# The start of a two-layer encoder kernel: first input half and first weights in two transfers each, idle TensorE on a zero tile, first half transposed in two parts

## Chip, core and metric

The kernel runs on one core of a Trainium2 chip. The metric is device time in microseconds (us) of one execution. Three runs of the kernel before gave 914.66, 915.12 and 915.35 us; their median, 915.12 us, is the time that the changed kernel is held against.

## What is computed

Two layers over x of 256 tokens by 1024 columns, fp32. Each layer has three sublayers, each followed by a layer norm of the scaled input plus the sublayer's output: a SwiGLU block, a mixer (chunked mLSTM in layer 0, windowed attention in layer 1), and a second SwiGLU block.

```python
for l in range(DEPTH):                                    # DEPTH = 2
    x = layer_norm(ALPHA * x + 0.5 * swiglu(x, ffn_w_in[l, 0], ffn_w_out[l, 0]), ln_g[l, 0], ln_b[l, 0])
    y = mlstm_mixer(x, ...) if l % 2 == 0 else window_attention(x, ...)
    x = layer_norm(ALPHA * x + y, ln_g[l, 1], ln_b[l, 1])
    x = layer_norm(ALPHA * x + 0.5 * swiglu(x, ffn_w_in[l, 1], ffn_w_out[l, 1]), ln_g[l, 2], ln_b[l, 2])
```

Only the first sublayer's beginning matters here: `x @ ffn_w_in[0, 0]`, whose right side has 1024 rows and 5632 columns.

## The kernel before

**Products.** The tokens are two tiles of 128: tile 0 and tile 1. TensorE needs x with its columns on the partitions, so each block of 128 tokens by 128 columns is transposed by a product with the identity (`ident`), and the result is copied out of PSUM. The eight column blocks are numbered k = 0 to 7; k 0 to 3 are the first half of x (columns 0 to 511) and k 4 to 7 the second.

To keep fp32 accuracy every operand is a pair: a high part rounded to fp32r (`xT_hi`, `w_hi`), and a low part that is the raw value less the high part (`xT_lo`, `w_lo`). A product is three matmuls: high by high, low by high, high by low. ScalarE (ACT) casts the high part of a weight piece, VectorE (DVE) subtracts to get the low part.

**Weights.** A piece is 256 rows by 512 columns (128 partitions by 1024 elements in SBUF, two k blocks), 512 KB. Pieces are numbered w0, w1, w2 and so on in order of use. SyncE (SP) issues their transfers through `Weights.load` (L221) and `Paced.load` (L109). There are four buffers (`RAW_BUFS`), so w4's transfer waits for the low part of w0 (`Weights.low`, L322), which frees its buffer.

**The start.** `load_x` (L574) loads x in four transfers of 256 KB, by token tile and half, all issued by ACT. SP issues w0 to w3 at the same time (L582 to L588). Then ACT loads its activation table (L589), and GpSimd's iota and a DVE compare make the identity (L593, L594).

`ffn` then records (L777 to L782): 14 transposes of the identity, whose results nobody reads (`warm`, L656); the four transposes of tile 0's first half, their copy to `xT_hi` and the subtraction for `xT_lo` on DVE (`to_xT`, L648); the split of w0 in two halves of 512 columns (L310 and L329); and eight more idle transposes.

`first_mm` (L802) orders the products of the first two pieces into the first PSUM bank pair, tile 0 and tile 1 of the tokens. For w0, in the order of the code: tile 0 high by `w_hi`; transposes of tile 1's first half; tile 0 low by `w_hi`; tile 0 high by `w_lo`; then the same three products of tile 1. Each of these is two matmuls of 128x512, one for each k block of the piece. For w1 the transposes of the second half of both token tiles come first, then again twelve matmuls. w2 and w3, which need the second half of x, follow through `b_mm` (L796), where each k block's three matmuls stand together, high by low second.

**What sets the order.** Each engine runs its instructions in the order in which they were recorded. `Paced` (L63) keeps a small model of the engines' and the transfers' times while it records; `Weights.fill` (L374) asks that model when to place the next cast or subtraction of a weight piece between other work. A change in the recorded loads or in the model's arrival times can therefore change the order of work on ACT and DVE.

Of the kernel before, what the change touches and what calls it, by code (L numbers as in the profile page):

```python
# [9 lines left out]
F32 = mybir.dt.float32  # L10
FR = mybir.dt.float32r
# [6 lines left out]
S = 256  # L18
# [20 lines left out]
XP = [4, 0, 1, 2]  # L39
LC = [0, 0, 0, 0, 0, 1]  # L40
TD = [2, 3, 2, 0, 2, 1]
MP = [1, 0, 0, 0, 1, 0, 1, 1, 0, 0, 0, 0, 2, 2, 2]
PD = [7, 0, 6, 6, 5]
PEND = [6, 4, 6, 6, 6]
# [9 lines left out]
ISSUING = 450.0  # L54
LANDING = 2200.0
LOADING = 1360.0
# [6 lines left out]
class Paced:  # L63
# [42 lines left out]
                self.there[ap.name][:a.size] = a  # L106
        self.there[ap.name][i] = t

    def load(self, ap, source, engine=None):  # L109
        if engine is not None:  # L110
            engine.dma_start(ap, source)
        elif isinstance(source, list):
            for k, src in enumerate(source):
                self.nc.sync.dma_start(ap[:, k].rearrange("p (m f) -> p m f", m=src.shape[1]), src)
        else:
            self.nc.sync.dma_start(ap, source)
        self.moving(0, ap, LANDING, LOADING * int(np.prod(ap.shape[1:])) / 1024, ISSUING)
# [69 lines left out]
class Weights:  # L187
# [33 lines left out]
    def load(self, most=None):  # L221

        nc = self.nc
        n = 0
        once = False
        while most is None or n < most:
            next_ = []
            for tag, todo in self.todo.items():
                if not todo:
                    continue  # L230
                first = self.first[todo[0]]
                if tag != "w_raw":
                    if self.free[tag] and not once and first < self.used + self.span:
                        next_.append((first, tag, tag))
                elif self.free[tag]:
                    next_.append((first, tag, tag))
                elif todo[0] < self.send and self.free["v_raw"]:
                    next_.append((first, tag, "v_raw"))
            if not next_:
                break  # L240
            _, tag, in_ = min(next_)
            once = once or tag != "w_raw"
            i = self.todo[tag].pop(0)
            pool, bufs = {"w_raw": (self.pool, RAW_BUFS), "v_raw": (self.spool, V_RAW)}.get(in_, (self.rooms, S_RAW))
            t = pool.tile([128, D], F32, name=tag, tag=in_, bufs=bufs)
            nc.load(t.rearrange("p (k f) -> p k f", k=self.words[i]["k"]), self.words[i]["src"])
            self.raw[i], self.words[i]["in"] = t, in_
            self.free[in_] -= 1
            n += 1
# [27 lines left out]
    def next(self, act):  # L277

        nc = self.nc
        free = RING - (len(self.made) - self.gone)  # L280
        i = self.first_left()
        best, need = None, 0
        for n in range(1, LOOK + 1):
            while i in self.made:
                i += 1
            if i >= len(self.plan) or need > free - 1:
                break
            p = self.plan[i]
            if (p["word"] in self.raw and nc.when(self.raw[p["word"]]) < act + SOON
                    and (p["needs"] is None or p["needs"] in self.made)  # L290
                    and not any(p["needs"] == x for x in [h[0] for h in self.half] + [s_[0] for s_ in self.sums])):
                if best is None or p["due"] < self.plan[best]["due"]:
                    best = i
            need = max(need, n - max(0, i - self.gone - n + 1 - KEPT))
            i += 1
        return best
# [146 lines left out]
def trunk_kernel(ctx: ExitStack, tc: tile.TileContext, x, ffn_w_in, ffn_w_out, ln_g, ln_b, ml_w_in, ml_gate_b,  # L443
                 ml_norm_g, ml_w_out, at_w_in, at_sink, at_w_out, out):
    nc = Paced(tc.nc)
    consts = ctx.enter_context(tc.tile_pool(name="consts", bufs=1))
# [78 lines left out]
    for j, (kind, l, i, _) in enumerate(stages):  # L525
        if kind == "ffn":
# [13 lines left out]
            for g in range(SEVENS):  # L540
                c0 = 768 + 512 * g
# [29 lines left out]

    xt = [state.tile([128, D], F32, name=f"x{t}", tag=f"x{t}") for t in range(2)]

    def load_x(t, h):  # L574
        s_ = slice(h * 512, h * 512 + 512)
        nc.load(xt[t][:, s_], x[0, t * 128:(t + 1) * 128, s_], nc.nc.scalar)

    xT = (state.tile([128, 8, S], FR, name="xT_hi", tag="xT_hi"),
          state.tile([128, 8, S], FR, name="xT_lo", tag="xT_lo"))

    W = Weights(nc, wpool, rooms, words, plan, after)
    load_x(0, 0)  # L582
    W.load(1)
    load_x(1, 0)
    W.load(1)
    load_x(0, 1)
    load_x(1, 1)
    W.load()  # L588
    nc.scalar.preload_act_table(AF.Silu)  # L589

    ident = consts.tile([128, 128], F32, name="ident")
# [28 lines left out]
    def pair(p, *idx):  # L620
        return p[0][idx], p[1][idx]
# [4 lines left out]
    def ybank(shape=(128, 512)):  # L626
        return psum.tile(list(shape), F32, name="py", tag="py", bufs=4)
# [3 lines left out]
    def tok(t):  # L631
        return slice(t * 128, (t + 1) * 128)

    def split_evac(dst, src, scale=None, high=None, wait=False):
        if scale is None:
            (high or nc.scalar.copy)(dst[0], src)
            low = lambda: nc.vector.tensor_sub(dst[1], src, dst[0].bitcast(F32))
            if wait:
                W.when_ready(low, dst[0])
            else:  # L640
                low()
        else:
            nc.scalar.activation(dst[0], src, AF.Copy, scale=scale)
            nc.vector.scalar_tensor_tensor(dst[1], src, scale, dst[0].bitcast(F32), op0=OP.mult, op1=OP.subtract)

    turned = {}

    def to_xT(t, src, bank, halves=range(2), high=None):  # L648
        for h in halves:
            p = bank((128, 4, 128))  # L650
            for k in range(4):
                nc.tensor.transpose(p[:, k], src[:, (4 * h + k) * 128:(4 * h + k + 1) * 128], ident)
            split_evac(pair(xT, A, slice(4 * h, 4 * h + 4), tok(t)), p, high=high)
            turned[t, h] = p

    def warm(n):  # L656

        p = ybank((128, 4, 128))
        for j in range(n):
            nc.tensor.transpose(p[:, j % 4], ident, ident)  # L660

    def load_ln(room, l, n):
        t = []
# [50 lines left out]
    def tail(y, h, todo, first, norm, last, turn_at, between=None, rooms_=None):  # L714
# [39 lines left out]
        if rooms_ is not None:  # L754
            norm[0].gb.clear()
            W.back(rooms_, 2)
        W.done(most=TD[bound[0]])
        W.owed, W.landed = 0, False
# [6 lines left out]
    def ffn(l, i, n, pending, last):  # L765
        with ExitStack() as ph:
# [9 lines left out]

            start = pending is None  # L777
            if start:
                warm(14)
                to_xT(0, xt[0], ybank, (0,), nc.vector.tensor_copy)  # L780
                W.split(1)
                warm(8)  # L782
            hs, pieces = [], []

            def tr(hB, t, h):
# [15 lines left out]

            def first_mm(ps, a):  # L802

                def mm(t, i, j):
                    for k in (2 * a, 2 * a + 1):
                        nc.tensor.matmul(ps[t], xT[i][:, k, tok(t)], pieces[a][j][:, k % 2], start=i == j == k == 0,
                                         stop=False)

                if a == 1:
                    for t in range(2):  # L810
                        to_xT(t, xt[t], ybank, (1,))
                pieces.extend(W.take(1))
                mm(0, 0, 0)
                if a == 0:
                    to_xT(1, xt[1], ybank, (0,))
                    W.split(2)
                mm(0, 1, 0)
                if a == 0:
                    mm(0, 0, 1)
                mm(1, 0, 0)  # L820
                if a == 0:
                    mm(1, 0, 1)
                mm(1, 1, 0)
                if a == 1:
                    mm(0, 0, 1)
                    mm(1, 0, 1)

# [39 lines left out]
            if start:  # L867
                sg = {}
                for m in range(2):
                    ps = [wbank(), wbank()]  # L870
                    for a in range(4):
                        if m == 0 and a < 2:
                            first_mm(ps, a)
                        for t in range(2):
                            if m or a > 1:
                                b_mm(ps[t], t, m, a)
                            if m == 1 and a == 3:
                                b_mul(sg[t], ps[t])
# [170 lines left out]
    def mlstm(l, n, pending, last):  # L1049
        with ExitStack() as ph:  # L1050
# [209 lines left out]

            pump = iter(MP)
            spare = lambda: W.done(0, next(pump))
# [351 lines left out]
```

## Time and profile before

| What | Value |
|---|---|
| Three timed runs | 914.66, 915.12, 915.35 us |
| The profiled execution's own time | 914.5 us |
| Its span in the profile | 912.8 us |
| Mean granted clock of TensorE | 0.999 |
| TensorE matmul busy | 903.3 us, 99% of the span, 4459 matmuls |
| VectorE busy | 804.5 us, 88% |
| ScalarE busy | 573.8 us, 63% |

How to read its rows. In the timeline the columns are start and duration in us from the span's start, engine, source line, operation, output<-inputs with shape, and the number of like instructions merged in the row; a bracket tells the engine's idle time before it and what ended that. PE is TensorE's matmuls, PEld its weight loads, ACTq and SPq the issuing of transfers. Most compute instructions pass through one wrapper and so carry its line, L178; they are told apart by the names of their tiles. A matmul's duration includes its way through the array, and the next one starts before it ends; the pitch, start to start, is what counts. In the rows of transfers the last figure is the time from issue to landing.

### The profile page before, as it was taken

How to read it: one execution, taken by the hardware profiler on the slowest of the kernel's cores; microseconds unless marked ns; L12 is line 12 of the kernel's file. 1: busy time of each engine (PE TensorE's matmuls, PEld its weight loads, DVE VectorE, ACT ScalarE, POOL GpSimd, SP SyncE). 2: the span in 40 equal slices, each digit the busy share in tenths (PEclk: the TensorE clock that was granted, in tenths of full speed). 3: DMA queues.
4: the chain of work that ended last, by engine and by line, in shares of the span. 5: the costliest groups of instructions: out<-in, count | busy, mean ns of one | idle time of the engine just before them, and what ended most of it. 6: DMA issues, size and time to landing. Idle time of an engine off the chain costs nothing.

```text
span 912.8 us, 12565 instructions
## 1 busy us (share of the span) xinstructions
PE 903.3 (99%) x4459; PEld 757.8 (83%) x4459; DVE 804.5 (88%) x969; ACT 573.8 (63%) x793; POOL 153.9 (17%) x194
## 2 busy tenths in 40 slices
PE   9999999999999999999999999999999999999996
PEld 7888888889988888888888888888888888888885
DVE  5999999886799898999888899998869889899986
ACT  5786767356664666776646676764569566676660
POOL 0111123013211011211011111110425301111110
PEclk9999999999999999999999999999999999999999
DMA  8999998546637898998868889985434487799851
GB/s 281 361 331 260 287 279 213 164 133 195 199 121 242 287 235 247 287 270 248 239 191 276 254 256 287 265 225 197 160 118 140 162 290 221 201 294 283 255 138 47
DMA packets 100703, 208.53 MB, mean 228 GB/s; under 512 B 6904, under 2 KB 21264, under 8 KB 100640
## 3 DMA queue, kind: packets, MB, share of 16 engines
q1 hardware_dynamic: 82368, 173.04, 54.0%
q0 software_dynamic: 17696, 33.65, 22.1%
q10 hardware_dynamic: 576, 1.05, 0.3%
q8 instruction: 35, 0.57, 0.2%
q14 instruction: 28, 0.23, 0.1%
HBM read 206.65 MB, written 1.05 MB: 228 GB/s over the span
## 4 chain that ended last, share of the span: by engine, by line
PE 95%; DVE 3%; issue 1%; POOL 1%; ACT 0%; DMA 0%; DVEq 0%; POOLq 0%; ACTq 0%
PE pw L178 61%; PE py L178 34%; DVE h L178 1%; POOL hrs L1237 0%; DVE w_lo L178 0%; DMA w_raw<-in_ml_w_out_dram 0%; DVE wt L178 0%; DVE x L178 0%; DVE hst L178 0%; ACT w_hi L178 0%; DVE stats L178 0%; DVE a_lo L178 0%; DVE hmv L178 0%; ACT a_hi L178 0%; DVE q_lo L178 0%
## 5 line engine op out<-in xcount | busy, mean ns | idle before, releaser
L178 DVE TENSOR_TENSOR w_lo<-w_raw,w_hi 128x1024 fp32r<-128x1024 f32 (+1 forms) x213 | 254.9, 1218 | 25.2 <-ACT w_hi L178 23.4
L178 ACT CAST w_hi<-w_raw 128x1024 fp32r<-128x1024 f32 (+1 forms) x213 | 219.0, 1050 | 76.8 <-PE py L178 21.9
L178 DVE TENSOR_TENSOR w_lo<-s_raw,w_hi 128x1024 fp32r<-128x1024 f32 x192 | 228.6, 1219 | 19.4 <-ACT w_hi L178 19.4
L178 ACT CAST w_hi<-s_raw 128x1024 fp32r<-128x1024 f32 x192 | 196.5, 1054 | 59.4 <-PE py L178 23.0
L178 PE MATMUL pw<-w_hi,xT_hi 128*128 128x512 f32 x480 | 189.3, 396 | 0.0
L178 PE MATMUL pw<-w_hi,xT_lo 128*128 128x512 f32 x480 | 186.8, 390 | 0.0
L178 PE MATMUL pw<-w_lo,xT_hi 128*128 128x512 f32 x480 | 186.6, 390 | 0.0
L120 POOL DMA_DIRECT2D s_raw<-in_ffn_w_in_dram x64 | 77.4, 1211 | 484.5 <-DVE s_raw L178 231.5
L178 PE MATMUL py<-w_hi,h_hi 128*128 128x512 f32 x349 | 138.1, 396 | 0.0
L178 PE MATMUL py<-w_hi,h_lo 128*128 128x512 f32 x349 | 136.1, 390 | 0.0
L178 PE MATMUL py<-w_lo,h_hi 128*128 128x512 f32 x349 | 135.8, 389 | 0.0
L178 PEld LDWEIGHTS pw<-w_hi,xT_lo 128*128 128x128 f32 x480 | 90.0, 188 | 19.1
L178 PEld LDWEIGHTS pw<-w_lo,xT_hi 128*128 128x128 f32 x480 | 90.3, 188 | 18.7 <-DVE w_lo L178 1.1
L178 PEld LDWEIGHTS pw<-w_hi,xT_hi 128*128 128x128 f32 x480 | 90.0, 188 | 17.3
L178 PE MATMUL pw<-w_hi,S_hi 128*128 128x512 f32 x256 | 99.6, 389 | 0.0
L178 PE MATMUL pw<-w_lo,S_hi 128*128 128x512 f32 x256 | 99.6, 389 | 0.0
L178 PE MATMUL pw<-w_hi,S_lo 128*128 128x512 f32 x256 | 99.6, 389 | 0.0
L178 PEld LDWEIGHTS py<-w_hi,h_lo 128*128 128x128 f32 x349 | 65.5, 188 | 14.1
L178 DVE TENSOR_TENSOR s_raw<-s_raw,s_raw 128x1024 f32<-128x1024 f32 x64 | 76.8, 1219 | 0.3
L178 PEld LDWEIGHTS py<-w_lo,h_hi 128*128 128x128 f32 x349 | 65.6, 188 | 12.9
L178 PEld LDWEIGHTS py<-w_hi,h_hi 128*128 128x128 f32 x349 | 65.6, 188 | 12.8
L178 PEld LDWEIGHTS pw<-w_hi,S_lo 128*128 128x128 f32 x256 | 48.0, 188 | 10.0
(203 smaller groups left out, 1128.9 us busy)
## 6 DMA issues: line engine op xcount, KB each, us to landing
s_raw<-in_ffn_w_in_dram SPq DMA_DIRECT2D x96, 512.0 KB, 7.9
w_raw<-in_ffn_w_out_dram SPq DMA_DIRECT2D x88, 512.0 KB, 6.0
w_raw<-in_ffn_w_in_dram SPq DMA_DIRECT2D x64, 512.0 KB, 5.5
s_raw<-in_ffn_w_in_dram POOLq DMA_DIRECT2D x64, 512.0 KB, 8.2
w_raw<-in_ml_w_in_dram SPq DMA_DIRECT2D x24, 512.0 KB, 4.4
w_raw<-in_ffn_w_in_dram SPq DMA_DIRECT2D x32, 256.0 KB, 5.8
w_raw<-in_at_w_in_dram SPq DMA_DIRECT2D x12, 512.0 KB, 4.4
w_raw<-in_ml_w_out_dram SPq DMA_DIRECT2D x8, 512.0 KB, 4.2
```

The source lines that it names most:

```text
L120: self.nc.gpsimd.dma_start(ap, source, accum_op=OP.add)
L178: r = f(out, *args, **kw)
```

## The change

- `load_x` takes columns and an engine. The first half of token tile 0 comes in two transfers of 256 columns (128 KB each), still issued by ACT. The other three quarters of x are now issued by SP, between the weights: w0, tile 1 first half, w1, tile 0 second half, w2, tile 1 second half, w3.
- w0 comes in two transfers of 256 KB, one for each k block.
- `warm` now does matmuls of 128x256 on a tile of zeros, `idle`, that DVE fills as its first instruction: 11 before the first transposes of x and 4 after them, in place of 14 and 8 transposes of the identity.
- The four transposes of token tile 0's first half are followed by two copies to `xT_hi` of two blocks each, and the subtraction for `xT_lo` is in two parts as well: k 0 and 1, then the low part of w0, then k 2 and 3.
- `first_mm` for w0: k 0 of tile 0 (high, low) by `w_hi`, then tile 1's transposes, then k 1, then the rest as before.

```diff
+WARM = [11, 4]
-    def load(self, ap, source, engine=None):
-        if engine is not None:
-            engine.dma_start(ap, source)
+    def load(self, ap, source, parts=False):
+        if parts:
+            for k in range(ap.shape[1]):
+                self.nc.sync.dma_start(ap[:, k], source[:, k])
...
-            nc.load(t.rearrange("p (k f) -> p k f", k=self.words[i]["k"]), self.words[i]["src"])
+            nc.load(t.rearrange("p (k f) -> p k f", k=self.words[i]["k"]), self.words[i]["src"], i == 0)
...
-    load_x(0, 0)
+    idle = consts.tile([128, S], FR, name="idle")
+    nc.vector.memset(idle.bitcast(F32), 0.0)
+    load_x(0, 0, 256, nc.nc.scalar)
+    load_x(0, 256, 512, nc.nc.scalar)
     W.load(1)
-    load_x(1, 0)
+    load_x(1, 0, 512, nc.nc.sync)
     W.load(1)
-    load_x(0, 1)
-    load_x(1, 1)
+    load_x(0, 512, 1024, nc.nc.sync)
+    W.load(1)
+    load_x(1, 512, 1024, nc.nc.sync)
     W.load()
...
-        p = ybank((128, 4, 128))
+        p = ybank((128, S))
         for j in range(n):
-            nc.tensor.transpose(p[:, j % 4], ident, ident)
+            nc.tensor.matmul(p, idle[:, 0:128], idle, start=True, stop=True)
...
-                warm(14)
-                to_xT(0, xt[0], ybank, (0,), nc.vector.tensor_copy)
-                W.split(1)
-                warm(8)
+                warm(WARM[0])
+                p = turned[0, 0] = ybank((128, 4, 128))
+                ks = slice(0, 2), slice(2, 4)
+                for k in range(4):
+                    nc.tensor.transpose(p[:, k], xt[0][:, k * 128:(k + 1) * 128], ident)
+                    if k % 2:
+                        nc.vector.tensor_copy(xT[0][:, ks[k // 2], tok(0)], p[:, ks[k // 2]])
+                warm(WARM[1])
+                W.high(0)
+                for i in range(2):
+                    nc.vector.tensor_sub(xT[1][:, ks[i], tok(0)], p[:, ks[i]], xT[0][:, ks[i], tok(0)].bitcast(F32))
+                    if i == 0:
+                        W.low()
...
                 if a == 0:
+                    mm(0, 0, 0, (0,))
+                    mm(0, 1, 0, (0,))
                     to_xT(1, xt[1], ybank, (0,))
                     W.split(2)
-                mm(0, 1, 0)
-                if a == 0:
+                    mm(0, 0, 0, (1,))
+                    mm(0, 1, 0, (1,))
                     mm(0, 0, 1)
-                mm(1, 0, 0)
-                if a == 0:
+                    mm(1, 0, 0)
                     mm(1, 0, 1)
-                mm(1, 1, 0)
+                    mm(1, 1, 0)
```

In the recorded programs, with the names of tiles alone compared, the instructions of TensorE, DVE, ACT and GpSimd stand in the same order in both kernels from the end of `first_mm`'s second piece on. At the start, beside what the diff says, one pair on ACT changes places: the cast of w2 (`w_hi`) stands before the copy of token tile 1's second half (`xT_hi`), where before it stood behind it. DVE's order there is unchanged: `xT_lo` of tile 0, `xT_lo` of tile 1, then `w_lo` of w2.

More of the change, by code (lines that the diff above doesn't have):

```diff
@@ L572, in trunk_kernel, with load_x @@
     xt = [state.tile([128, D], F32, name=f"x{t}", tag=f"x{t}") for t in range(2)]
-    def load_x(t, h):
-        s_ = slice(h * 512, h * 512 + 512)
-        nc.load(xt[t][:, s_], x[0, t * 128:(t + 1) * 128, s_], nc.nc.scalar)
+    def load_x(t, c0, c1, engine):
+        engine.dma_start(xt[t][:, c0:c1], x[0, t * 128:(t + 1) * 128, c0:c1])
+        nc.moving(0, xt[t][:, c0:c1], LANDING, LOADING * (c1 - c0) / 1024, ISSUING)
     xT = (state.tile([128, 8, S], FR, name="xT_hi", tag="xT_hi"),
@@ L802, in first_mm, with mm @@
             def first_mm(ps, a):
-                def mm(t, i, j):
-                    for k in (2 * a, 2 * a + 1):
+                def mm(t, i, j, ks=(2 * a, 2 * a + 1)):
+                    for k in ks:
                         nc.tensor.matmul(ps[t], xT[i][:, k, tok(t)], pieces[a][j][:, k % 2], start=i == j == k == 0,
@@ L812, in first_mm @@
                 pieces.extend(W.take(1))
-                mm(0, 0, 0)
                 if a == 0:
+                    mm(0, 0, 0, (0,))
+                    mm(0, 1, 0, (0,))
                     to_xT(1, xt[1], ybank, (0,))
                     W.split(2)
-                mm(0, 1, 0)
-                if a == 0:
+                    mm(0, 0, 0, (1,))
+                    mm(0, 1, 0, (1,))
                     mm(0, 0, 1)
-                mm(1, 0, 0)
-                if a == 0:
+                    mm(1, 0, 0)
                     mm(1, 0, 1)
-                mm(1, 1, 0)
-                if a == 1:
+                    mm(1, 1, 0)
+                else:
+                    mm(0, 0, 0)
+                    mm(0, 1, 0)
+                    mm(1, 0, 0)
+                    mm(1, 1, 0)
                     mm(0, 0, 1)
```

## Prediction

> **What bounds the kernel now.** I read the page first: its span and the chain of work that ended last. Then I read TensorE's waits, to learn where along that chain it stands still.
>
> ```profile
> span 912.8 us, 12565 instructions
> ...
> PE 95%; DVE 3%; issue 1%; POOL 1%; ACT 0%; DMA 0%; DVEq 0%; POOLq 0%; ACTq 0%
> ```
>
> ```profile
> PE py L178 <- DVE ident L178: 1.7, 1, 1.7
> PE py L178 <- DVE w_lo L178: 0.6, 1, 0.6
> PE pw L178 <- DVE q_lo L178: 0.2, 1, 0.2
> ```
>
> The reader is to see that TensorE is the bound nearly everywhere: 95% of the chain is its work, and of the waits that the matmuls show, 1.7 us lie before the first matmul and only 0.6 + 0.2 us anywhere else. So what the start gains or loses reaches the end of the run nearly undiminished, and nothing else can gain much, since the instructions after the start stand in the same order. The profiled execution took 914.5 us, 1.7 more than its span and 0.6 less than the median of 915.12; I work out a shift in the span and apply it to the median.
>
> Next the timeline of the start, for the work that isn't useful.
>
> ```profile
> 0.79 2.14 ACTq L111 DMA_DIRECT2D x<-in_x_dram  x4
> 0.80 14.90 SPq L116 DMA_DIRECT2D w_raw<-in_ffn_w_in_dram  x8
> ...
> 1.43 0.23 DVE L178 TENSOR_SCALAR ident<-ji 128x128 f32<-128x128 int32 x1 [1.43 <-POOL ji L593]
> ...
> 1.72 3.25 PE L178 MATMUL py<-ident 128*128 128x128 f32 x14 [1.72 <-DVE ident L178]
> ...
> 4.76 1.06 PE L178 MATMUL py<-ident,x 128*128 128x128 f32 x4
> ...
> 5.61 1.33 PE L178 MATMUL py<-ident 128*128 128x128 f32 x8
> ```
>
> From 1.72 to 6.7 us TensorE does only idle transposes and the first four of x. The early ones are slow: 14 in 3.25 us is 0.23 each. The later rows show what comes after the start, up to the last place where TensorE waits for a weight there.
>
> ```profile
> 10.25 1.04 PE L178 MATMUL py<-ident,x 128*128 128x128 f32 x8
> 11.04 0.71 PE L178 MATMUL pw<-w_hi,xT_hi 128*128 128x512 f32 x2
> ...
> 10.89 1.07 ACT L178 CAST xT_hi<-py 128x512 fp32r<-128x512 f32 x2 [0.86 <-PE py L178]
> 11.85 2.95 ACT L178 CAST w_hi<-w_raw 128x1024 fp32r<-128x1024 f32 x3
> ...
> 11.51 1.29 DVE L178 TENSOR_TENSOR xT_lo<-py,xT_hi 128x512 fp32r<-128x512 f32 x2 [0.22 <-ACT xT_hi L178]
> 12.94 3.50 DVE L178 TENSOR_TENSOR w_lo<-w_raw,w_hi 128x1024 fp32r<-128x1024 f32 x3
> ...
> 13.86 0.39 PE L178 MATMUL pw<-w_hi,xT_hi 128*128 128x512 f32 x1
> 14.22 0.50 PE L178 MATMUL pw<-w_lo,xT_hi 128*128 128x512 f32 x1
> ```
>
> The eight transposes of x's second half start at 10.25. Eight take 1.04 us, 0.13 each: the fast pitch. w1's twelve matmuls run from 11.04 to 13.86, 0.235 each. w2's first matmul is at 13.86, and the next would follow 0.23 later, at 14.09, but stands until 14.22 for w2's low part. I call this instruction **the landmark**: its start shifts as the end does.
>
> **The change, part by part.** The transfers come first, because all else waits for them.
>
> ```profile
> x<-in_x_dram ACTq DMA_DIRECT2D x1, 256.0 KB, 3.7
> 1.25 0.45 ACTq L111 DMA_DIRECT2D x<-in_x_dram  x1
> x<-in_x_dram ACTq DMA_DIRECT2D x1, 256.0 KB, 5.2
> 2.21 0.72 ACTq L111 DMA_DIRECT2D x<-in_x_dram  x1
> x<-in_x_dram ACTq DMA_DIRECT2D x1, 256.0 KB, 7.9
> w_raw<-in_ffn_w_in_dram SPq DMA_DIRECT2D x1, 512.0 KB, 4.6
> 1.81 0.46 SPq L116 DMA_DIRECT2D w_raw<-in_ffn_w_in_dram  x1
> w_raw<-in_ffn_w_in_dram SPq DMA_DIRECT2D x1, 512.0 KB, 9.0
> ```
>
> ```profile
> 2.20:2.70 0.50, 0.50 (x4) 1.00 0.77 180
> 10.20:11.20 1.00, 1.00 (x10) 1.00 1.08 385
> ```
>
> In order these are the first, second and fourth transfer of x and the first and third of the weights, each issue's start ahead of its size and time to landing (the first issues are at 0.79 and 0.80, above). They landed at 4.5 (tile 0 first half), 6.5 (tile 1 first half), 10.1 (tile 1 second half), 5.4 (w0) and 10.8 (w2). The last two rows are windows with TensorE's busy time, its granted clock, and the transfers' share and GB/s.
>
> *First part of x, 128 KB.* Not later than 4.5, where all 256 KB landed; not earlier than 3.8, since 128 KB at the 180 GB/s of that time are 0.7 us. I take 4.0. The second part lies between 4.5 and w0's 5.4; I take 4.8. w0's halves I put at 4.7 and 5.6, the sum of the bytes being what it was.
>
> *Tile 1 first half.* The 768 KB ahead of it landed by 5.4. With the engines to itself it needs 0.65 us more at 385 GB/s: 6.05. At worst it stays about where it was, or pays 0.4 for two more transfers: 6.9. I take 6.3.
>
> *Tile 1 second half.* This one loses. It used to share the engines with w2 and landed ahead of it; now it is queued behind w2. All bytes but w3's, 2.5 MB, had landed at 10.8, so it should be there by 10.8; if the single queue runs at 385 GB/s throughout and w3's bytes stay behind, by 10.1. I take 10.4. The row at 10.20 is one in which SP's queue was alone, so one queue can run at that rate. SP's more issues at about 0.5 us each put this transfer's issue near 4 us, five before its bytes are due, so they cost nothing. ACT's two fewer issues only move its idle time.
>
> *TensorE's early work.* DVE's memset has no row; ident's 0.23 us for half the elements is below it, the DVE row of 256 columns next is above.
>
> ```profile
> L178 DVE TENSOR_TENSOR q_lo<-pw,q_hi 128x256 fp32r<-128x256 f32 x8 | 3.4, 422 | 1.8 <-ACT q_hi L178 1.8
> ```
>
> ```profile
> 699.87 1.60 PE L178 MATMUL pw<-pr,v 128*128 128x256 f32 x12
> ```
>
> From about 0.8, when the other engines issue, it ends at 1.1 (1.0 to 1.25), and TensorE starts 0.6 us earlier. A fast 128x256 matmul is 0.13 us (twelve in 1.60); slow by 0.23/0.13 it is 0.235, so eleven end at 3.7, ahead of the first part of x: hidden. The first two transposes are at 4.05; the next two wait for the second part of x, 4.85 to 5.3. The four idle matmuls end at 5.8 to 6.2.
>
> *DVE.* The second copy is at 5.35, 0.42 long, and the low part of k 0 and 1 is ready at 6.15. The halves of w0's low part follow to 7.4 (the cast of the second half is done at 6.2), the low part of tile 1 by 8.4 (ready at 9.2 before). Four DVE instructions of 256 columns for two of 512 add some 0.15 us, covered, since none of these is awaited by TensorE at that time.
>
> *First block.* k 0's two matmuls start at 6.0 and 6.25; tile 1's transposes at 6.45, 0.1 after their data; then 4 x 0.11 + 10 x 0.23 = 2.75 us with nothing late. The block, and so the start of the eight transposes, call it T, is at 9.2 instead of 10.25: **1.05 us earlier**.
>
> *From T to the landmark.* Here most of that goes again, by two paths. Through TensorE: tile 1's transposes can't start before its second half has landed at L: L + 0.05, four transposes 0.44, twelve matmuls 2.75, one more 0.23: L + 3.45 = 13.85 for L = 10.4. Through ACT and DVE: w2's cast now stands ahead of tile 1's copy. From T: 0.64 to ACT's start (10.25 to 10.89), a copy 0.48 (two until 11.85), the cast 0.98 (2.95/3), tile 1's copy 0.59, DVE's two steps 0.6 and 1.2, and hand-overs 0.1: T + 4.6 = 13.8; before it was 14.22 - 10.25 = 3.97. So the swap gives back 0.6 of what T gains. The later path is at 13.85 against 14.22: **0.37 us earlier, -0.4 us in all**.
>
> After that the transfer of w4, awaiting w0's low part, is issued some 1.1 us earlier, as w0's is done earlier; the later waits of TensorE (0.8 us in all) bound what else can move, either way.
>
> **Rivals.**
>
> *The late quarter.* Tile 1's second half lands after 10.8. TensorE is in order, so w1's matmuls stand behind transposes whose results only w2 needs. Beyond 10.77 the kernel is slower, us for us: at 11.3 by 0.5. For it: seven transfers in one queue, while the first transfers' rate was 180 GB/s. Against: 385 GB/s with one queue. This is the rival on the slower side.
>
> *The slow pitch lasts.* 0.23 turns to 0.13 while the eight idle transposes run, near 6.0, with no gap in TensorE's work since 1.72; the granted clock reads 1.00 throughout, so that column doesn't tell of it. The change makes gaps, for each part of x. If the turn comes at R instead of 6, T is (R - 6)/2 later; beyond R = 6.9 the gain is gone, and at R = 9.4 the kernel is 1.2 us slower. The Trainium skill ("TensorE: Matmul & The Clock Gate", Part 1) says that the clock rises after a busy window of about 3.4 us that runs freely, so the turn may come up to a window later; the row of 14 fits that and can't show where the window lies. The same page's Part 4 has it that transposes don't count as busy; here only transposes had run when the pitch turned, so the trace disagrees.
>
> *More comes through.* Tile 1 at 6.0 and its second half at 10.0 give T = 8.9 and a landmark of 13.5, 0.7 earlier; better by more than 1 us would need the 4.6 us behind T to shrink.
>
> *The parts don't land earlier.* If the first transfers are limited by their start, x's parts come at 4.5 and 5.4: k 0's low part is at 6.75, T 0.6 later, 9.8, and the landmark at 14.4: 0.2 slower.
>
> **How the numbers follow.** The forecast is -0.4 on 915.12: 914.7. I give it 0.5 (between -0.7 and -0.1), the late quarter 0.2, the slow pitch 0.1, parts that don't land earlier 0.1, more gain 0.1. The range takes in the gain of 0.7 and the loss of 0.5, and most of the slow pitch's, and the 0.35 us by which runs shown stray from their median: 913.8 to 916.0. A measurement of this kernel can tell about 0.2%, 1.8 us, from no change. No case reaches that by itself: faster 0.05, same 0.90, slower 0.05.
>
> **What would show it.** The first idle matmul near 1.1; transposes of x in two pairs from 4.0; w0's first matmul near 6.0; eight transposes from 9.2, with a gap between the two tiles'; ACT's cast of w2 ahead of tile 1's copy; the landmark (w2's second matmul) at 13.85. I am wrong if the pitch is still 0.2 after 6.5, if tile 1's second half lands after 10.8, or if later stages shift by more than the landmark does.

## The result, and the profile after

| | before | after |
|---|---|---|
| Median of 7 runs | 914.94 us | 917.65 us |
| Lowest to highest | 914.57 to 915.55 | 916.26 to 918.25 |
| The profiled execution's own time | 914.5 | 918.25 |
| Its span | 912.8 | 916.5 |

The changed kernel is slower: by the medians 2.7 us. The ratio of the runs is 1.0024, 95% interval 1.0015 to 1.0034, that is 1.4 to 3.1 us. Repeated (kernel 11 below) it was 917.34 against 914.62, ratio 1.0031, 1.0021 to 1.0042. The forecast was 0.4 us faster, and the range ended at 916.0.

The head of the page after and the shares of its chain, to be set beside those of before:

```profile
span 916.5 us, 12558 instructions
...
PE 93%; DVE 4%; issue 1%; ACT 1%; POOL 0%; DMA 0%; DVEq 0%; ACTq 0%; POOLq 0%
```

TensorE's longest waits after (the figures are us in total, times, and the longest in us):

```profile
PE py L180 <- DVE idle L180: 1.2, 1, 1.2
PE pw L180 <- DVE w_lo L180: 1.1, 2, 0.6
PE py L180 <- DMA x<-in_x_dram: 0.9, 1, 0.9
PE py L180 <- DVE xT_hi L180: 0.5, 1, 0.5
PE py L180 <- DVE w_lo L180: 0.2, 1, 0.2
```

TensorE starts half a microsecond earlier (1.2 for 1.7), but two new waits stand behind that: 0.9 us for x's first part and 0.5 us for DVE's copy of it. Waits for `w_lo` grew from 0.6 to 1.3 us. These rows alone give 2.1 us of new waits less 0.5; they don't show the greater loss, which is in the timeline of TensorE's matmuls:

```profile
1.25 2.71 PE L180 MATMUL py<-idle 128*128 128x256 f32 x11 [1.25 <-DVE idle L180]
4.83 0.66 PE L180 MATMUL py<-ident,x 128*128 128x128 f32 x2 [0.88 <-DMA x<-in_x_dram]
6.02 0.69 PE L180 MATMUL py<-ident,x 128*128 128x128 f32 x2 [0.52 <-DVE xT_hi L180]
6.36 1.20 PE L180 MATMUL py<-idle 128*128 128x256 f32 x4
...
9.92 1.05 PE L180 MATMUL pw<-w_lo,xT_hi 128*128 128x512 f32 x2
10.77 1.02 PE L180 MATMUL pw<-w_hi,xT_hi 128*128 128x512 f32 x2
11.62 0.62 PE L180 MATMUL pw<-w_lo,xT_hi 128*128 128x512 f32 x2
...
12.55 1.03 PE L180 MATMUL py<-ident,x 128*128 128x128 f32 x8
...
17.11 0.50 PE L180 MATMUL pw<-w_lo,xT_hi 128*128 128x512 f32 x1 [0.55 <-DVE w_lo L180]
```

Read the pitch, row start to row start. Two matmuls of 512 columns take 0.85 us from 9.92 to 10.77 and from 10.77 to 11.62, 0.43 each; the pair from 11.62 is over in 0.62, its last one's way through the array included, where the pair before takes 1.02; from there on they take 0.23 each. So TensorE runs at half its pace until about 11.5, where before it turned near 6.0. T, the start of the eight transposes, is at 12.55 for 10.25, and the landmark at 17.11 for 14.22: 2.9 us later, about what the runs show. (The two spans differ by 3.7; the 0.8 us beyond the landmark are scatter. From the landmark to the end of the span it is 898.6 us before and 899.4 after, and 898.4 to 900.3 in the profiles of the experiments, with single waits of 0.2 to 1 us for `w_lo` that come and go.)

The windows answer (busy time and count of each engine, then granted clock, transfers' share, GB/s) over the two paces:

```profile
8.00:11.00 3.00, 3.00 (x10) 2.41 (x10) 1.86 (x5) 1.53 (x2) 0.00 (x0) 1.00 1.06 385
...
12.00:13.00 1.00, 1.00 (x9) 0.83 (x8) 0.09 (x1) 0.00 (x0) 0.00 (x0) 1.00 0.33 123
```

Ten matmuls in three microseconds, then nine in one, with about as many short ones in both, and the granted clock reads 1.00 in both: that column and the busy share don't show the slow pitch. Only the pitch does.

### The profile page after: what moved, and what is told of

It is laid out like the page before. It is cut to its first block, busy times and chain, and to the rows that moved or that the text cites. A ratio compares the mean times of both kernels' runs of the same rounds, so it can differ in the third digit from the quotient of the medians.

```text
span 916.5 us, 12558 instructions
## 1 busy us (share of the span) xinstructions
PE 905.0 (99%) x4452; PEld 758.5 (83%) x4452; DVE 805.1 (88%) x972; ACT 573.3 (63%) x793; POOL 153.4 (17%) x194
## 4 chain that ended last, share of the span: by engine, by line
PE 93%; DVE 4%; issue 1%; ACT 1%; POOL 0%; DMA 0%; DVEq 0%; ACTq 0%; POOLq 0%
PE pw L180 60%; PE py L180 32%; DVE w_lo L180 1%; DVE h L180 1%; POOL hrs L1256 0%; DMA x<-in_x_dram 0%; ACT w_hi L180 0%; DVE wt L180 0%; DVE x L180 0%; DVE hst L180 0%; ACT xT_hi L180 0%; DVE stats L180 0%; DVE e L180 0%; DVE s_raw L180 0%; DVE a_lo L180 0%
## 5 line engine op out<-in xcount | busy, mean ns | idle before, releaser
L180 PEld LDWEIGHTS pw<-w_hi,S_hi 128*128 128x128 f32 x256 | 48.1, 188 | 10.0
```

The lines of the kernel that those rows point to most:

```text
L180: r = f(out, *args, **kw)
```

## The experiments

All kernels were timed in five rounds beside the kernel before on the same chip; "above" is the difference of the medians. The last slow matmul, T and the landmark are from each one's single profile. The last slow matmul is given by the start of the last one that went at the slow pace for at least a part. It is read from single matmuls in the same traces: in a merged row the first matmul of a new kind takes longer at either pace (the first idle one of 128x256 behind transposes 0.20 us at the fast pace, 0.36 at the slow one). Medians of kernels on one chip that lie within 0.5 us are not told apart: runs of one kernel spread over 2 us.

**The theory**: the slow pitch ends only after TensorE has worked for some microseconds without a pause; the 0.9 us pause ahead of x's first part starts that anew. **Rivals**: idle matmuls on zeros don't count as work; the transfers or the swapped cast are the loss; the second pause (0.5 us) is the one that counts.

**1. The zero tile alone, no pause.**

```diff
 # in the kernel before
+    idle = consts.tile([128, S], FR, name="idle"); nc.vector.memset(idle.bitcast(F32), 0.0)
-            nc.tensor.transpose(p[:, j % 4], ident, ident)
+            nc.tensor.matmul(p, idle[:, 0:128], idle, start=True, stop=True)
-                warm(14)
+                warm(16)
```

> The kernel before, with only the idle work changed: matmuls on the zero tile, 16 and 8 of them, sized so that TensorE has no pause before the first half of x. Pause theory (the slow pitch lasts because TensorE stood idle for 1.1 and 0.5 us before the transposes of x): no pause, so the pitch turns before about 8 us as in the kernel before, and the time is within 0.5 us of 914.9. Zero theory (work on a tile of zeros does not bring the fast pitch): the pitch is still slow beyond 8.5 us and the time is 1.5 to 2.5 us above. Order theory (only the late data and the new order cost time): same as before, pitch as before.

Measured: 914.61 against 914.55, ratio 0.9997 (0.9988 to 1.0006). Its timeline of TensorE:

```profile
1.25 3.53 PE L178 MATMUL py<-idle 128*128 128x256 f32 x16 [1.25 <-DVE idle L178]
4.70 0.63 PE L178 MATMUL py<-ident,x 128*128 128x128 f32 x4
5.08 1.20 PE L178 MATMUL py<-idle 128*128 128x256 f32 x8
```

The eight later idle matmuls go at 0.14 each (w0's first matmul follows at 6.20). The four transposes ahead of them are fast too, 0.38 us from 4.70 to 5.08. Of the sixteen earlier idle matmuls the last slow one, at 0.20 to 0.21, starts at 4.2. So work on zeros turns the pitch as the transposes do. The zeros are not the loss.

**2. A pause alone.** The kernel before with 9 idle transposes for 14, nothing else.

```diff
-                warm(14)
+                warm(9)
```

> The kernel before with 9 idle transposes in place of 14, so that TensorE stands idle for some 0.9 us before the first half of x lands; nothing else differs and the useful work starts when it did. Pause theory: the pitch turns only between about 8 and 11.5 us in place of 6, and the time rises by 1 to 2.3 us. Zero theory and order theory: no change, within 0.4 us of 914.9.

Measured: 915.28 against 914.55, ratio 1.0011 (1.0002 to 1.0019). Its eleven runs lie in two groups, six at 914.6 to 915.3 and five at 915.8 to 917.7. The profiled run is one of the second:

```profile
1.71 2.18 PE L178 MATMUL py<-ident 128*128 128x128 f32 x9 [1.71 <-DVE ident L178]
4.99 1.12 PE L178 MATMUL py<-ident,x 128*128 128x128 f32 x4 [1.09 <-DMA x<-in_x_dram]
5.90 1.91 PE L178 MATMUL py<-ident 128*128 128x128 f32 x8
...
9.17 0.81 PE L178 MATMUL pw<-w_hi,xT_lo 128*128 128x512 f32 x2
9.82 0.63 PE L178 MATMUL pw<-w_lo,xT_hi 128*128 128x512 f32 x2
```

Five fewer idle transposes leave a pause of 1.09 us, and the eight later ones still take some 0.2 each (1.91 for the eight); the turn is at 9.2 to 9.6 and the landmark at 15.66. A pause by itself moved the turn by 3 us in this run. Whether the two groups of runs are a late and an early turn isn't shown: kernel 13 below, without a pause, has two such groups as well. The median is 0.7 us up, less than the 1 to 2.3 us that the text on record gave the theory.

**3. The changed kernel without its pauses**: 17 idle matmuls ahead, and the four later ones between the two pairs of transposes, in a bank of their own.

```diff
 # in the changed kernel
-WARM = [11, 4]
+WARM = [17, 4]
-                warm(WARM[0])
+                idle_to = ybank((128, S))   # fill_in(n): n matmuls of idle into it
+                fill_in(WARM[0])
...
+                    if k == 2:
+                        fill_in(WARM[1])
-                warm(WARM[1])
```

> The changed kernel with its pauses filled: 17 idle matmuls on the zero tile before x and 4 between the two pairs of transposes. Pause theory: the pitch turns before about 8 us, the eight transposes start near 10.3 instead of 12.55, the time falls by about 2 us to 915.6, still some 0.6 above the kernel before because of the cast that stands ahead of the copy on ScalarE. Zero theory and order theory: 917.6, no change within 0.5.

Measured: 915.69 against 914.55, ratio 1.0012 (1.0003 to 1.0021): of the 2.7 us, 1.6 are gone.

```profile
1.24 3.86 PE L180 MATMUL py<-idle 128*128 128x256 f32 x17 [1.24 <-DVE idle L180]
4.94 0.41 PE L180 MATMUL py<-ident,x 128*128 128x128 f32 x2
5.10 0.72 PE L180 MATMUL py<-idle 128*128 128x256 f32 x4
...
6.08 0.47 PE L180 MATMUL pw<-w_hi,xT_hi 128*128 128x512 f32 x1
7.17 0.50 PE L180 MATMUL pw<-w_hi,xT_lo 128*128 128x512 f32 x1 [0.62 <-DVE xT_lo L180]
```

The turn comes early again, before 4.94: the first two transposes of x take 0.41, where the changed kernel's take 0.66. What is late now is x: w0's first matmul starts at 6.08, near the 6.0 of the prediction, but the next waits 0.62 us for `xT_lo`, T is at 10.27 and the landmark at 14.84.

**4. The changed kernel with the old idle work**, 9 and 4 transposes of the identity, its pauses kept (0.86 and 0.52 us).

```diff
-            nc.tensor.matmul(p, idle[:, 0:128], idle, start=True, stop=True)
+            nc.tensor.transpose(p[:, j % 4], ident, ident)
-WARM = [11, 4]
+WARM = [9, 4]
```

> The changed kernel with transposes of the identity as idle work, 9 and 4, so that the pause before x is as long as in the changed kernel. Pause theory: slow pitch as in the changed kernel, 917.6 within 0.7. Zero theory: pitch turns near 6 us and the time falls by about 2 us to 915.6. Order theory: 917.6.

Measured: 918.03 against 914.55, ratio 1.0035 (1.0023 to 1.0048); last slow matmul at 10.7, landmark at 16.78. No faster than the changed kernel: with the pauses kept, idling on transposes instead of zeros doesn't help.

**5. The filled kernel with ACT's old order** (w2's cast behind tile 1's copy).

```diff
 # in kernel 3, around the turning of x's second half
+                    held, nc.filler = nc.filler, None
                     for t in range(2):
                         to_xT(t, xt[t], ybank, (1,))
+                    nc.filler = held
```

> The filled kernel (changed kernel with its pauses filled) with the old order on ScalarE: the cast of w2 behind the copy of tile 1's second half. Order theory for the 1.1 us that were left: from the eight transposes to the landmark 4.0 us in place of 4.57, landmark near 14.3 in place of 14.84, 0.5 to 0.6 us faster than the filled kernel, so 0.5 above the kernel before. Late-data theory (what is left comes from the later landing of x alone): no change from the filled kernel, 1.1 above the kernel before.

Measured: 915.95 against 915.00, ratio 1.0011 (1.0002 to 1.0020). T is at 10.89 and the landmark at 14.87, 3.98 behind it, where the swapped order has 4.57 in kernel 3. So the swap does cost 0.6 us behind T; the run as a whole gains nothing that can be told, since here T itself was later (the turn came at 6.6).

**6. The new transfers alone**, on kernel 1, with 21 idle matmuls so that no pause arises; x's first half is turned as one.

```diff
 # in kernel 1: load_x, W.load(1) and the loads in parts as in the change
-                warm(16)
+                warm(21)
```

> The kernel before with zero-tile idle work (21 and 8 matmuls, no pause) and only the transfers of the changed kernel; x's first half is turned in one part, as before. Late-data theory: the first transposes of x start at 5.8 in place of 4.7, the eight transposes at 10.4 to 10.9, and with the swapped cast that these transfers bring the landmark is at 15.0 to 15.5: 0.8 to 1.3 us slower than the kernel before. Turning theory (the transfers are harmless, the turning in two parts costs): within 0.3 of the kernel before.

Measured: 916.12 against 915.00, ratio 1.0012 (1.0003 to 1.0021). x's second part landed at 5.77, T is at 10.87, the landmark at 15.43.

**7. The turning in parts alone**: kernel 3 with the transfers of before (16 idle matmuls ahead).

```diff
 # in kernel 3: load_x, W.load(1) and the loads as before the change
-WARM = [17, 4]
+WARM = [16, 4]
```

> The filled kernel with the transfers of the kernel before: zero-tile idle work, x's first half turned in two parts and the new order of w0's products, no pause, no swapped cast. Late-data and order theories: the eight transposes at 9.5 to 9.9, landmark 4.0 later, time within 0.4 us of the kernel before, perhaps 0.3 below. Turning theory: 0.7 to 1.1 us slower than the kernel before.

Measured: 915.71 against 915.00, ratio 1.0011 (1.0001 to 1.0022), with runs from 914.3 to 918.6. x's first half landed at 5.21 in the profiled run, which left a pause of 0.32. The transposes right behind the pause are fast already, and the last slow matmul, ahead of it, starts at 4.6; the landmark is at 14.65. The time is at the edge of what the text gives the turning theory, but x came 0.7 us later here than in the kernel before, so the price of turning in parts isn't shown.

**8. The second pause alone**: the changed kernel with 17 idle matmuls for 11.

```diff
-WARM = [11, 4]
+WARM = [17, 4]
```

> The changed kernel with 17 idle matmuls, so that the pause before x is filled and only the one of some 0.5 us between the two pairs of transposes is left. If a pause of 0.5 us is enough to hold the slow pitch: turn beyond 8.5 us and 917 to 918, as in the changed kernel. If only the longer pause counts: as the filled kernel, 1.1 us above the kernel before.

Measured: 915.98 against 915.00, ratio 1.0012 (1.0003 to 1.0021).

```profile
1.25 3.99 PE L180 MATMUL py<-idle 128*128 128x256 f32 x17 [1.25 <-DVE idle L180]
5.04 0.63 PE L180 MATMUL py<-ident,x 128*128 128x128 f32 x2
6.18 0.44 PE L180 MATMUL py<-ident,x 128*128 128x128 f32 x2 [0.52 <-DVE xT_hi L180]
6.38 0.72 PE L180 MATMUL py<-idle 128*128 128x256 f32 x4
```

The 0.52 us pause stays, and the pitch has turned by its end all the same: the pair of transposes at 5.04 took 0.63, the pair at 6.18 takes 0.44. Six idle matmuls more, and nothing else, take the loss from 2.7 to 1.0 us. The second pause is not what counts; the next kernel, which lacks it, shows the same from the other side.

**9. The first pause alone**: kernel 3 with 11 idle matmuls ahead. **10. The same with none ahead.** **11. The changed kernel again.** These three ran on one chip.

```diff
 # 9, in kernel 3
-WARM = [17, 4]
+WARM = [11, 4]
 # 10, in kernel 3
-WARM = [17, 4]
+WARM = [0, 4]
```

> The changed kernel with the four later idle matmuls put between the two pairs of transposes (in a bank of their own), eleven idle matmuls ahead as before: of its two pauses, the first (some 0.9 us before x's first part) stays, the second (0.5 us) is filled. Theory (the pitch turns 3.5 to 5 us after the start of a run without pause, and a pause of about 1 us starts that anew): slow matmuls until 8.3 to 9.7, landmark 15.5 to 16.5, time 916.3 to 917.3. Rival (the second pause is the one that counts, or both together): turn near 5 to 6, landmark 14.8 to 15.2, time 915.5 to 916, as with both filled.

> As the kernel with only its first pause left, but without any idle matmul ahead of x: TensorE's first work is the first pair of transposes, near 4.8. Theory (work ahead of a pause of about 1 us is lost): the same turn, 8.3 to 9.7, and the same time within 0.5 us, 916.3 to 917.3. Rival (slow work adds up, whether or not pauses lie in it): the eleven idle matmuls' 2.4 us are missing, so the turn comes later by up to 2.4 us and the time is longer by up to 1.2 us than with them.

> The changed kernel again, on the chip of the two above, for a comparison on one chip. Both theories: 917 to 918, slow matmuls until 10 to 11.5, landmark 16.5 to 17.2.

Measured, against 914.62: kernel 9 917.87, ratio 1.0036 (1.0023 to 1.0048); kernel 10 917.65, 1.0029 (1.0018 to 1.0039); kernel 11 917.34, 1.0031 (1.0021 to 1.0042). Kernel 9's timeline:

```profile
1.25 2.71 PE L180 MATMUL py<-idle 128*128 128x256 f32 x11 [1.25 <-DVE idle L180]
4.85 0.66 PE L180 MATMUL py<-ident,x 128*128 128x128 f32 x2 [0.89 <-DMA x<-in_x_dram]
...
8.23 0.95 PE L180 MATMUL py<-ident,x 128*128 128x128 f32 x4
8.93 0.47 PE L180 MATMUL pw<-w_hi,xT_hi 128*128 128x512 f32 x1
```

and kernel 10's:

```profile
4.83 0.66 PE L180 MATMUL py<-ident,x 128*128 128x128 f32 x2 [4.83 <-DMA x<-in_x_dram]
...
10.77 0.99 PE L180 MATMUL pw<-w_hi,xT_hi 128*128 128x512 f32 x2
11.59 0.62 PE L180 MATMUL pw<-w_lo,xT_hi 128*128 128x512 f32 x2
```

The first pause alone brings the whole loss, and by the times a kernel with no idle matmul at all ahead of x is as fast as one with eleven. So the eleven idle matmuls bought nothing that the times show: the pause behind them made their 2.7 us worthless.

The rival by which slow work adds up across a pause has kernel 10 up to 1.2 us behind kernel 9. In the two single profiles it is: the last slow matmul is at 8.9 in kernel 9 and 11.2 in kernel 10, and the landmarks are 1.2 us apart. But the medians don't differ so, and the changed kernel and kernel 11, with eleven idle matmuls, have their last slow matmul at 11.2 and 10.8, as late as kernel 10 with none. So the rival has no support in the times; that early work is worth a few tenths of a microsecond isn't excluded. The turns spread more widely than the text on record allowed for, and kernel 9's time is 0.6 above what it said.

**12. w0 in halves alone**, on kernel 1.

```diff
 # in kernel 1: load(..., parts=i == 0) as in the change, for w0 only
```

> The kernel before with idle matmuls on the zero tile (16 and 8, no pause), and of the change's transfers only one: w0 in two halves of 256 KB; x comes whole in 256 KB pieces from ACT as before. Theory A (the split of x's first half into two transfers on one queue is what brings it late): here x's first half lands near 4.6 whole, w0's halves at 4.5 to 4.8 and 5.5, w0's first matmul is at or ahead of 6.2, the landmark 13.3 to 13.8, time within 0.5 us of the kernel before. Theory B (any further transfer ahead in these queues delays the rest): x's first half lands at 5.2 or later, the landmark is at 14.3 or later, time 0.5 us or more above the kernel before.

Measured: 915.72 against 914.64, ratio 1.0009 (1.0000 to 1.0018). x's first half landed at 5.16, the landmark is at 14.31. That is the second theory's side, but kernels 7 and 15 had x at 5.2 as well without a split of w0, so one profile doesn't prove it.

**13 to 15. The last microsecond.** About 1 us was left in each kernel with filled pauses but not in kernel 1, so kernel 1 was run again on one chip with two more single steps on top of it: x's first half in two transfers, and x's other quarters on SP.

```diff
 # 14 (x's halves), in kernel 1
-    load_x(0, 0)
+    load_x(0, 0, 256, nc.nc.scalar)
+    load_x(0, 256, 512, nc.nc.scalar)
-                warm(16)
+                warm(20)
 # 15 (x's queue), in kernel 1
-    load_x(1, 0)
+    load_x(1, 0, 512, nc.nc.sync)
     W.load(1)
-    load_x(0, 1)
-    load_x(1, 1)
+    load_x(0, 512, 1024, nc.nc.sync)
+    W.load(1)
+    load_x(1, 512, 1024, nc.nc.sync)
```

> The kernel before with idle matmuls on the zero tile (16 and 8), again, on the chip of the two below. Theory A (the last 1 us comes from the transfers and from the turning in parts): within 0.4 us of the kernel before, landmark 13.7 to 14.4. Theory B (it comes with the zero tile or with any edit, and the first comparison missed it): 0.7 us or more above the kernel before.

> The same, with 20 idle matmuls ahead, and x's first half in two transfers of 128 KB from ACT, turned as one; the other quarters, w0 and the order of the queues as before. Theory A: both parts are there at 5.5 to 5.8, 1 us later than whole, so landmark 14.6 to 15.2 and 0.7 to 1.2 us above the kernel before. Theory B: as the zero tile alone.

> The zero tile alone (16 and 8), with x's other three quarters issued by SP between the weights as the change does; x's first half and w0 whole. Theory A: x's first half lands at 4.5 to 4.7, tile 1's first half near 6.3; w2's cast may stand ahead of tile 1's copy, which gives back 0.6 us behind the eight transposes: landmark 13.9 to 14.6, 0 to 0.6 us above the kernel before. Theory B: as the zero tile alone.

Measured, against 914.67: the zero tile again 915.37, ratio 1.0007 (0.9998 to 1.0015); x's halves 916.06, 1.0011 (1.0002 to 1.0020); x's queue 915.34, 1.0009 (1.0000 to 1.0017). Kernel 14's first two transfers of x, the issue of the first at 0.8 and the median of both:

```profile
x<-in_x_dram ACTq DMA_DIRECT2D x1, 128.0 KB, 3.3
...
x<-in_x_dram ACTq DMA_DIRECT2D x2, 128.0 KB, 3.8
```

The first part landed at 4.11, the second at 5.62; turned as one, x waits for the second, T is at 11.17 and the landmark at 15.14, as the first theory has it; the time, 1.4 above, is 0.2 beyond its range. Kernel 15's x landed at 5.20 though nothing ahead of it was changed, and its landmark at 15.23 is beyond what either text allowed. The zero tile's 0.06 on the first chip is 0.70 here, with intervals that overlap; by the text on record 0.7 is just on the side of the second theory, by which the loss comes with the zero tile or with any edit. Kernel 13's twelve runs lie in two groups, six at 914.2 to 914.8 and six at 915.9 to 917.0.

| Kernel | Pause ahead of x, us | Last slow matmul | T | Landmark | Above before, us |
|---|---|---|---|---|---|
| before | none | 6.0 | 10.25 | 14.22 | |
| 1, 13 zero tile | none | 4.2, 6.7 | 9.81, 10.44 | 13.78, 14.42 | 0.1, 0.7 |
| 2 pause alone | 1.09 | 9.2 | 11.69 | 15.66 | 0.7 |
| 3 filled | none | 4.6 | 10.27 | 14.84 | 1.1 |
| 5 filled, old order | none | 6.6 | 10.89 | 14.87 | 1.0 |
| 6 transfers | none | 5.7 | 10.87 | 15.43 | 1.1 |
| 7 turning in parts | 0.32 | 4.6 | 10.67 | 14.65 | 0.7 |
| 8 second pause | none | 5.2 | 10.57 | 15.14 | 1.0 |
| 12 w0 in halves | 0.27 | 4.6 | 10.35 | 14.31 | 1.1 |
| 14 x's halves | none | 6.7 | 11.17 | 15.14 | 1.4 |
| 15 x's queue | 0.30 | 5.8 | 10.66 | 15.23 | 0.7 |
| 4 old idle work | 0.86 | 10.7 | 12.21 | 16.78 | 3.5 |
| 9 first pause | 0.89 | 8.9 | 11.35 | 15.92 | 3.3 |
| 10 none ahead | 4.83 (no work before) | 11.2 | 12.51 | 17.08 | 3.0 |
| after, 11 | 0.88, 0.91 | 11.2, 10.8 | 12.55, 12.39 | 17.11, 16.95 | 2.7, 2.7 |

The table parts at one column. Where the pause ahead of x is at most 0.32 us, the last slow matmul starts at 4.2 to 6.7 and the kernel is 0.1 to 1.4 us above before. At 0.86 us and more it starts at 8.9 to 11.2, and the kernel is 2.7 to 3.5 us above, but for kernel 2 with 0.7.

**Shown**: the first pause costs 1.6 to 1.7 us of the 2.7 (what kernels 3 and 8 lack of the changed kernel's loss, by the medians), and with it alone the loss is whole (9 and 10). The intervals overlap at their edges (1.0003 to 1.0021 for kernels 3 and 8, 1.0015 to 1.0034 and 1.0021 to 1.0042 for the changed kernel), but kernels 3, 5 and 8 are all 1.0 to 1.1 us above, and the changed kernel, twice, and kernels 4, 9 and 10 all 2.7 to 3.5. **Open**: the last microsecond. x in two transfers has the largest of the single steps (1.4), but the steps' prices lie within each other's intervals and don't add up (1.1 for all transfers, 1.1 for transfers and parts), and kernel 13 has 0.7 by the zero tile alone, so it is not shared out here. One term can be seen in the table: where x's other quarters come from SP and ACT's order is swapped, the landmark is 4.56 to 4.57 behind T, elsewhere 3.96 to 3.98. That a version would beat the kernel before is not in sight: the best landmark, kernel 1's, is 0.4 us early, and its two medians are 0.1 and 0.7 above.

## Why the prediction was wrong, point by point

**The step that failed: "eleven end at 3.7, ahead of the first part of x: hidden".** The end was about right: 3.95, by the wait of 0.88 us ahead of 4.83. But an end ahead of x is a pause, and a pause was what could not be afforded. I costed the idle matmuls by what they delay, which is nothing, and not by what they are for: keeping TensorE busy until its pitch turns. The step that rests on it, the first block's "4 x 0.11 + 10 x 0.23", took the fast pitch for all of it; the block's matmuls up to 11.5 went at 0.43.

**The rival "The slow pitch lasts" was this mechanism, with the wrong weight and too short a reach.** It had 0.1, and its worst case was a turn at 9.4. Its formula, T later by (R - 6)/2, holds: R = 11.4 gives 2.7, and the parts' lateness 0.6 (the formula of "The parts don't land earlier"), so T = 9.2 + 2.7 + 0.6 = 12.5; measured 12.55. That it fits so closely is partly luck, since the parts came 0.2 to 0.3 us later still than that rival has them. Two rivals that I held apart came together. The page of the Trainium skill that stood beside it ("TensorE: Matmul & The Clock Gate", Part 1) has the activity window free-running. I take from that that a pause may spoil the window that it falls into and cost up to another, and the runs fit it: from the end of the pause to the last slow matmul 4.0 us in kernel 9, 6.4 in kernel 10, which starts there. Kernel 1's first fast matmul starts 3.1 us after its first matmul, sooner than the busy window of about 3.4 us that the prediction takes from this page of the Trainium skill; there the measurement decides. The advice of the same page of the Trainium skill ("Why this matters for your kernels"), no idle gaps over about 3 us between bursts of matmuls, is given for the middle of a kernel and doesn't cover the time ahead of the turn: here 0.9 us was enough.

**x's parts: 4.0 and 4.8 forecast, 4.70 and 5.68 measured.** The answer on transfers after, one row for each issue with its time to landing, and the issues' starts:

```profile
x<-in_x_dram ACTq DMA_DIRECT2D x1, 128.0 KB, 3.9
0.79 0.41 ACTq L577 DMA_DIRECT2D x<-in_x_dram  x1
...
x<-in_x_dram ACTq DMA_DIRECT2D x1, 128.0 KB, 4.4
1.24 0.46 ACTq L577 DMA_DIRECT2D x<-in_x_dram  x1
```

Half the bytes took 3.9 us from issue, where the whole 256 KB had taken 3.7. My lower bound, bytes by the GB/s of that time, took the rate for one queue's; w0's halves, issued at the same moment, landed at 4.48 and 5.45 and shared it. The rival that has the parts at 4.5 and 5.4 was the nearer one, and even it was 0.2 to 0.3 early.

**A wait that I overlooked: the second pair of transposes behind DVE's copy of the first.** DVE's rows after:

```profile
0.92 0.27 DVE L180 MEMSET idle<- 128x256 f32 x1 [0.92 <-PEq L1620]
...
5.54 0.42 DVE L180 CAST xT_hi<-py 128x256 fp32r<-128x256 f32 x1 [3.88 <-PE py L180]
6.74 0.42 DVE L180 CAST xT_hi<-py 128x256 fp32r<-128x256 f32 x1 [0.78 <-PE py L180]
```

x's second part was there at 5.68, but the pair started at 6.02, when the copy (5.54 to 5.96) had left the tile of PSUM that both pairs share. I had "the next two wait for the second part of x" only. By kernel 8 this second pause is worth nothing that the runs can tell. The idle tile's memset ended at 1.19, in the range given; TensorE's start at 1.25 gained 0.47 us for the forecast 0.6.

**Right: w0's halves** (4.7 and 5.6 forecast, 4.48 and 5.45), **tile 1's halves** (6.3 and 10.4 forecast, 6.25 and 10.32), so the late quarter didn't happen. **Right: the path behind T, "T + 4.6".** ACT's and DVE's rows after:

```profile
13.18 0.58 ACT L180 CAST xT_hi<-py 128x512 fp32r<-128x512 f32 x1 [2.35 <-PE py L180]
13.66 1.05 ACT L180 CAST w_hi<-w_raw 128x1024 fp32r<-128x1024 f32 x1
14.61 0.59 ACT L180 CAST xT_hi<-py 128x512 fp32r<-128x512 f32 x1
```

```profile
15.23 0.69 DVE L180 TENSOR_TENSOR xT_lo<-py,xT_hi 128x512 fp32r<-128x512 f32 x1 [0.74 <-ACT xT_hi L180]
15.84 3.49 DVE L180 TENSOR_TENSOR w_lo<-w_raw,w_hi 128x1024 fp32r<-128x1024 f32 x3
```

w2's cast (13.66) stands between the two copies, DVE waits 0.74 us for the second, and `w_lo` is ready when the landmark starts: 17.11 - 12.55 = 4.56, against 3.97 before and 3.98 in kernel 5 with the old order.

**The chances.** The forecast's 0.4 us was smaller than the price of the one thing that every microsecond of the start hangs on, and that price had no upper bound in the trace of before, which has no pause. A rival whose size the trace couldn't bound, with "I am wrong if the pitch is still 0.2 after 6.5" written beside it, deserved more than 0.1.

**A small misreading: the slow pitch, 0.23.** It was taken from a row's whole duration, 14 in 3.25; start to start it is 0.21. Nothing rests on it, since the first idle matmul takes longer: the eleven took 2.71 us for the 2.6 of the forecast.

## What to carry to other kernels

Idle work at the start of a kernel is there to run into the first real work without a long pause; here 0.9 us was too long and 0.3 was not. Count it until the data lands at its latest, not until it lands as hoped: six idle matmuls more put the first transposes of x 0.2 us later (5.04 for 4.83) and took 1.7 us off the loss. When a profile's busy share and granted clock look the same, compare the start-to-start time of like matmuls to see which pace the engine runs at. And a smaller first transfer need not be an earlier one while another queue loads at the same time (4.70 in the changed kernel, 4.11 in kernel 14, 4.47 for the whole before): bound its landing by that of the whole, from its issue.

## What the runs showed of the hardware

- The pitch of a matmul of 512 columns is 0.43 us ahead of the turn and 0.23 behind it; of 128x256 ones on the idle tile 0.213 and 0.12; the granted clock reads 1.00 for both.
- A pause of 0.86 to 1.09 us ahead of the turn moved the last slow matmul from 4.2 to 6.7 out to 8.9 to 11.2. A pause of 0.30 us there did not (kernel 15), nor did pauses of 0.27, 0.32 and 0.52 us with slow matmuls before and fast ones right behind (kernels 12, 7 and 8), nor one of 0.62 us behind the turn (kernel 3).
- The last slow matmul started 4.0 to 6.4 us after the end of a pause of 0.86 us or more (or the first work, in kernel 10), and 2.9 to 5.5 us after the first matmul in kernels without a pause. One kernel can differ by 2.5 us in this: kernels 1 and 13 are the same one on two chips, with 4.2 and 6.7.
- Transfers at the start: x's first half landed whole at 4.47 to 5.21 in seven profiles with the transfer unsplit; in two parts the first landed at 4.66 to 4.80 (once at 4.11) and the second at 5.62 to 5.81, later than any whole one.
